# State tiles by twos and fours, attention heads by pairs, and the scaling of the weights on ScalarE, in a two-block model on one core

## The chip, the cores and the metric

The kernel runs on one core of a Trainium2 chip. A core has TensorE (PE in the profile, its weight loads PEld), VectorE (DVE), ScalarE (ACT), GpSimdE (POOL) and SyncE (SP), which here issues the transfers. The metric is the time of one execution on the device in microseconds (us); lower is better.

## The reference, cut to what matters

Two transformer blocks on 256 tokens of width 2048, one after the other. The change touches two parts of the second block's mixer, a diagonal state-space layer (64 groups of 16 channels, 64 complex states each) and an attention of 16 heads of 64 in four groups with three branches:

```python
def _s5(u, a_re, a_im, log_dt, b_re, b_im, c_re, c_im, d_skip):
    ...
    bu_re = jnp.einsum('btgc,gpc->tbgp', ug, bb_re)
    bu_im = jnp.einsum('btgc,gpc->tbgp', ug, bb_im)
    ...
    _, _, x_re, x_im = lax.associative_scan(_ssm_combine, (a_r, a_i, bu_re, bu_im), axis=0)
    y = (jnp.einsum('tbgp,gcp->btgc', x_re, c_re)
         - jnp.einsum('tbgp,gcp->btgc', x_im, c_im)
         + d_skip.reshape(SSM_GROUPS, SSM_GROUP) * ug)

def _nsa(q, kc_raw, vc_raw, ks_raw, vs_raw, kw_raw, vw_raw, g_logits, ...):
    k_cmp = _compress(kc_raw, cmp_pos, ck_w1, ck_w2)
    v_cmp = _compress(vc_raw, cmp_pos, cv_w1, cv_w2)
    ...
        o_c = jnp.einsum('bghqk,bkgd->bqghd', p_c.astype(v_cmp.dtype), v_cmp)
        ...
        p_s = _masked_softmax(s_s, (dist_s >= 0)[:, :, None])
        o_s = jnp.einsum('bghqk,bgqkd->bqghd', p_s.astype(vg.dtype), vg)
        ...
        p_w = _masked_softmax(s_w, valid_w)
        o_w = jnp.einsum('bghqk,bkgd->bqghd', p_w.astype(vwb.dtype), vwb)
        return gb[..., 0:1] * o_c + gb[..., 1:2] * o_s + gb[..., 2:3] * o_w
```

## The kernel before, in words

**The linears.** Every large product streams its weights in chunks of 512 KB (`chunk`, line 300): SP loads `wr` (4 buffers), ScalarE casts it to `wh` (3 buffers), VectorE subtracts and writes the residual `wl` (2 buffers). A chunk serves 24 matmuls of a full 128x128 array and 256 columns (high part by high part, residual by high, high by residual). After each chunk `linear` calls `background()`, which adds a share to every generator in the background and advances it a step when the sum reaches one. These matmuls read `wh` and `wl` with activations `r`, `m`, `hh` or `hl`; all matmuls go through `mm` and so have line 290 in before and 291 in the changed kernel.

**The state-space layer** (`s5`) runs in the background of the linears kv_in2, q_in2, gn_in2 and ga_in2 at 0.48 steps per chunk, 32 units j, one per step. A unit has two input matmuls with 32 rows of the array (`m,bt` in the profile, 256 columns, into a PSUM tile), six VectorE operations of 512 elements and two scans (`w<-ps,tab`, `w<-w,w`, `w<-mag,w`, `w<-w,tab`), and two steps later two output matmuls into 32 columns of the array (`w,cc`). Four units share the array's four row groups and column groups of 32, and one PSUM tile of outputs.

**The attention** (`nsa`) begins with the compressed branch: `compress` adds positions (`t<-m,params` and `t<-sw,params`, `sw` being a copy of the raw keys with the halves exchanged) and multiplies its own streamed weights. Then come 32 units, one head and branch each, at 0.75 steps per chunk behind the linears ga_in2, glu2 and gb_in2: `scores` (two matmuls on 64 rows, `m,m`; then VectorE's bias, maximum and sums, ScalarE's exponentials `w<-w,nm`, and VectorE's scaling `w<-w,sm` at line 282), two steps later `turn` (three transposes `eye,w` at line 1622 and a ScalarE copy to `pt`, which is `w<-ps 128x384`), and two steps after that `values` (two matmuls into 64 columns, `w,vt`; at a head's first branch also one on 15 rows, `pct,vcm`).

**What sets the order.** Each engine runs its instructions in one fixed order. The Tile scheduler decides that order from the program's order and its own model, so a step does not stand in one piece on an engine: instructions of a linear can stand between its matmuls. In the mixer, tiles `w` rotate in a ring of 11, `bt`, `cc`, `sw` and `tab` in rings of 2, PSUM tiles in 8 banks. A write into a ring's oldest buffer waits for its last reader.

Of the kernel before, what the change touches and what calls it, by code (L numbers as in the profile page):

```python
# [7 lines left out]
F32 = mybir.dt.float32  # L8
F32R = mybir.dt.float32r
ACT = mybir.ActivationFunctionType  # L10
ALU = mybir.AluOpType
# [3 lines left out]
P = 128  # L15
T = 256
# [4 lines left out]
EPS = 1e-6  # L21
NEG = -1e30
CH = 1024

# [202 lines left out]
class Builder:  # L227
# [1143 lines left out]
    def s5(self, pm, M, u):  # L1371
        nc = self.nc
        new = self.new
        sw = lambda a: a[:, ::-1]
        tiles = {}

        def load(c):
            bt = new(pm, "bt", [P, 2, P], F32, 2)
            nc.sync.dma_start(bt, self.d_bt[:, :, c * P:(c + 1) * P])
            cc = new(pm, "cc", [P, 2, P], F32, 2)  # L1380
            nc.sync.dma_start(cc[:, 0], self.ap["c_re"][:, c * P:(c + 1) * P])
            nc.sync.dma_start(cc[:, 1], self.ap["c_im"][:, c * P:(c + 1) * P])
            nc.gpsimd.tensor_scalar(out=cc[:, 1], in0=cc[:, 1], scalar1=-1.0, scalar2=None, op0=ALU.mult)
            tiles[c] = bt, cc

        def load_tab(j):

            tab = new(pm, "tab", [P, 3, T], F32, 2)
            nc.sync.dma_start(tab[:, 0:2], self.d_tab[j])
            self.act(tab[:, 2], tab[:, 1], ACT.Copy, scale=-1.0)  # L1390
            tiles["t", j] = tab

        def inputs(j):
            c, i = j // 4, j % 4
            sl = slice(32 * i, 32 * i + 32)
            bt = tiles[c][0]
            tab = tiles.pop(("t", j))
            cs = tab[:, 0:1].to_broadcast([P, 2, T])
            bu = self.ps()
            self.mm(bu[:, 0], bt[sl, 0], u[c][sl], True, True)  # L1400
            self.mm(bu[:, 1], bt[sl, 1], u[c][sl], True, True)
            p, r = new(pm, "w", [P, 2, T], F32, 11), new(pm, "w", [P, 2, T], F32, 11)
            self.tt(p, bu, cs, ALU.mult)
            self.tt(r, sw(bu), tab[:, 1:3], ALU.mult)
            self.tt(p, p, r, ALU.add)
            z = new(pm, "w", [P, 2, T], F32, 11)
            mg = self.mag[:, j:j + 1].to_broadcast([P, T])
            for k in range(2):
                nc.vector.tensor_tensor_scan(z[:, k], mg, p[:, k], 0.0, op0=ALU.mult, op1=ALU.add)
            x, r = new(pm, "w", [P, 2, T], F32, 11), new(pm, "w", [P, 2, T], F32, 11)  # L1410
            self.tt(x, z, cs, ALU.mult)
            self.tt(r, sw(z), tab[:, 2:0:-1], ALU.mult)
            self.tt(x, x, r, ALU.add)
            tiles["x", j] = x

        def outputs(j):
            c, i = j // 4, j % 4
            sl = slice(32 * i, 32 * i + 32)
            if i == 0:
                tiles["y"] = self.ps()[:, 0]  # L1420
            psy, cc, x = tiles["y"], tiles[c][1], tiles.pop(("x", j))
            self.mm(psy[sl], cc[:, 0, sl], x[:, 0], True, False, True)
            self.mm(psy[sl], cc[:, 1, sl], x[:, 1], False, True, True)
            if i < 3:
                return None
            y = self.t1()
            d = self.par("ssm_d_2")
            self.stt(y, u[c], d[:, c:c + 1], psy, ALU.mult, ALU.add)
            self.act(y, y, ACT.Gelu_apprx_tanh)
            hi, lo = M(F32R), M(F32R)  # L1430
            self.split(y, hi, lo)
            return hi, lo

        load(0)
        load_tab(0)
        for j in range(34):
            res = outputs(j - 2) if j >= 2 else None
            if j % 4 == 2 and j < 30:
                load(j // 4 + 1)
            if j < 31:  # L1440
                load_tab(j + 1)
            if j < 32:
                inputs(j)
            yield res

    def nsa(self, pm, M, q, kv, gates, onsa):
        nc, ap = self.nc, self.ap
        new = self.new
        kc, vc, ks, vs, kw, vw = (kv[2 * n:2 * n + 2] for n in range(6))
# [6 lines left out]
        ps = self.ps()  # L1456
# [35 lines left out]
        for which, raw in (("k", kc), ("v", vc)):  # L1492
# [1 line left out]
            hid = self.ps()[0:60, 0]  # L1494
            pos = self.par("cmp_pos_2")

            sw = new(pm, "sw", [P, 2, T], F32, 2)
            for t in range(2):
                nc.sync.dma_start(sw[64:128, t], raw[t][0:64])
                nc.sync.dma_start(sw[0:64, t], raw[t][64:128])  # L1500
# [77 lines left out]
                self.act(pct[j][:, sl], tp[:, j], ACT.Copy)  # L1578
        yield

        units = [(m, a, br) for m in range(8) for a in range(2) for br in range(2)]
        held = {}

        def scores(n):
            m, a, br = units[n]
            hi = (m % 4) * 4 + 2 * (m // 4) + a
            ds = slice(64 * a, 64 * a + 64)
            if br == 0:
                bias = new(pm, "w", [P, 3, P], F32, 11)

                nc.sync.dma_start(bias[:, 0], self.hankel(hi, P))
                nc.sync.dma_start(bias[:, 1:3].rearrange("p a b -> p (a b)"), self.hankel(hi, T))
                held["bias"] = bias
            bias = held["bias"]
            k = (ks, kw)[br][m // 4]
            ps = self.ps().rearrange("p a (b c) -> p (a b) c", c=P)
            self.mm(ps[:, 0:2].rearrange("p a b -> p (a b)"), q[m][ds, P:T], k[ds], True, True)
            self.mm(ps[:, 2], q[m][ds, 0:P], k[ds, 0:P], True, True, True)
            s = new(pm, "w", [P, 3, P], F32, 11)
# [12 lines left out]
            self.tt(sm, sm, gates[:, :, 16 * (br + 1) + hi], ALU.mult)  # L1612
            self.ts(s[:, 0:2], s[:, 0:2], sm[:, 1:2], None, ALU.mult)
            self.ts(s[:, 2], s[:, 2], sm[:, 0:1], None, ALU.mult)
            held["s", n] = s

        def turn(n):
            s = held.pop(("s", n))
            tp = self.ps().rearrange("p a (b c) -> p (a b) c", c=P)

            for b, src in enumerate((2, 0, 1)):
                nc.tensor.transpose(tp[:, b], s[:, src], self.eye)  # L1622
            pt = new(pm, "w", [P, 3, P], F32, 11)
            self.act(pt, tp[:, 0:3], ACT.Copy)
            held["p", n] = pt

        def values(n):
            m, a, br = units[n]
            g = 2 * (m // 4) + a
            ds = slice(64 * a, 64 * a + 64)  # L1630
            if a == 0 and br == 0:
                held["o"] = self.ps()[:, 0]
            o = held["o"]
            if br == 0:
                gs = slice(32 * g, 32 * g + 15)
                self.mm(o[ds], vcm[gs], pct[m % 4][gs], True, False, True)
            pt, vt = held.pop(("p", n)), vts[br]
            gc = slice(g * 64, g * 64 + 64)
            self.mm(o[ds], vt[:, 0, gc], pt[:, 0:2].rearrange("p a b -> p (a b)"), False, False, True)
            self.mm(o[ds, P:T], vt[:, 1, gc], pt[:, 2], False, br == 1, True)  # L1640
            if a == 1 and br == 1:
                hi, lo = M(F32R), M(F32R)
                self.split(o, hi, lo)
                onsa.append((hi, lo))

        for n in range(len(units) + 4):
            if n >= 4:
                values(n - 4)
            if 2 <= n < len(units) + 2:
                turn(n - 2)  # L1650
            if n < len(units):
                scores(n)
            yield

    def hankel(self, head, n):
# [46 lines left out]
```

## Time and profile before

| | |
|---|---|
| median of 3 runs | 3635.79 us (3632.27 to 3638.65) |
| the profiled execution | 3634.55 us |
| its span, first to last instruction | 3632.8 us |
| TensorE's granted clock, mean | 0.990 of full speed |
| TensorE busy | 3554.9 us |
| VectorE busy | 2220.6 us |
| ScalarE busy | 1580.4 us |

The span is what the profiler saw between the first and last instruction; 1.75 us lie around it. Busy times overlap between engines. The two parts that change lie between about 2116 and 2640 us of the span: the state-space layer up to some 2420 us, the attention's units behind it.

### The profile page before, as it was taken

The page shows a single profiled execution, that of the slowest core. Times are in us where ns is not written, and L with a number is a line of the kernel's source. Part 1 is how long each engine was busy: PE and PEld are TensorE (multiplying, and loading weights), DVE is VectorE, ACT ScalarE, POOL GpSimd, SP SyncE. Part 2 cuts the span into 40 slices and gives each one's busy share as a digit, 9 for nine tenths or more (in the row PEclk, how much of TensorE's full clock was granted, in tenths as well). Part 3 has the DMA queues.
Part 4 walks back from the last instruction along what each step waited for, and adds up shares of the span by engine and source line. Part 5 has one row for each costly group of instructions (what it writes and reads, how often), then busy time and mean ns, then how long its engine had stood idle before and what let it go on. Part 6 is the DMA issues. An engine that isn't in the chain of part 4 may idle for free.

```text
span 3632.8 us, 67934 instructions
## 1 busy us (share of the span) xinstructions
PE 3554.9 (98%) x28264; PEld 3372.4 (93%) x28264; DVE 2220.6 (61%) x3210; ACT 1580.4 (44%) x2033; POOL 20.0 (1%) x65
## 2 busy tenths in 40 slices
PE   8999999999999999999999899999999999999998
PEld 4788899999999999999999888888899899999997
DVE  2564367676655489865544689876656755555445
ACT  2433345454444444444434433455544544444333
POOL 0000000000000000000000000000000000000000
PEclk9999999999999999999999999999999999999999
DMA  9886857676555556765555555544455455555554
GB/s 340 312 287 215 289 187 231 220 229 214 184 182 185 182 188 221 225 197 185 182 185 181 165 167 176 163 150 126 122 177 185 151 186 181 185 182 184 182 184 140
DMA packets 213318, 710.83 MB, mean 196 GB/s; under 512 B 23904, under 2 KB 39296, under 8 KB 213008
## 3 DMA queue, kind: packets, MB, share of 16 engines
q1 hardware_dynamic: 213008, 706.48, 59.9%
q8 instruction: 221, 3.62, 0.4%
q14 instruction: 89, 0.73, 0.1%
HBM read 694.29 MB, written 11.57 MB: 194 GB/s over the span
## 4 chain that ended last, share of the span: by engine, by line
PE 94%; DVE 3%; DMA 1%; ACT 1%; issue 1%; SPq 0%; ACTq 0%; DVEq 0%
PE ps L290 93%; DVE wl L275 1%; DVE r L278 1%; DVE t L275 0%; PE ps L1622 0%; DMA wr<-in_w_qk_in 0%; DVE w L275 0%; DMA r<-in_xT 0%; DMA wr<-in_w_ada 0%; ACT wh L272 0%; DVE r L275 0%; DMA tab<-d_tab 0%; DVE t L278 0%; DMA wa<-in_w_qk_in 0%; DMA wa<-in_w_ada 0%
## 5 line engine op out<-in xcount | busy, mean ns | idle before, releaser
L275 DVE TENSOR_TENSOR wl<-wr,wh 128x1024 fp32r<-128x1024 f32 x1064 | 1300.6, 1223 | 1105.7 <-PE ps L290 869.4
L272 ACT ACTIVATE wh<-wr 128x1024 fp32r<-128x1024 f32 x1064 | 1127.0, 1059 | 1569.5 <-PE ps L290 1406.2
L290 PE MATMUL ps<-r,wh 128*128 128x256 f32 x12224 | 1759.9, 285 | 28.1 <-ACT r L272 22.0
L290 PEld LDWEIGHTS ps<-r,wh 128*128 128x128 f32 x12224 | 1592.7, 192 | 70.6 <-ACT r L272 28.4
L290 PE MATMUL ps<-r,wl 128*128 128x256 f32 x6112 | 998.4, 285 | 9.0 <-DVE wl L275 8.9
L290 PEld LDWEIGHTS ps<-r,wl 128*128 128x128 f32 x6112 | 847.8, 192 | 26.0 <-issue 12.3
L290 PE MATMUL ps<-hh,wl 128*128 128x256 f32 x2112 | 345.0, 283 | 0.0
L290 PE MATMUL ps<-hl,wh 128*128 128x256 f32 x2112 | 345.0, 283 | 0.0
L290 PE MATMUL ps<-hh,wh 128*128 128x256 f32 x2112 | 343.9, 283 | 0.0
L290 PEld LDWEIGHTS ps<-hh,wl 128*128 128x128 f32 x2112 | 294.0, 192 | 0.0
L290 PEld LDWEIGHTS ps<-hl,wh 128*128 128x128 f32 x2112 | 294.0, 192 | 0.0
L290 PEld LDWEIGHTS ps<-hh,wh 128*128 128x128 f32 x2112 | 293.4, 192 | 0.0
L290 PE MATMUL ps<-m,wh 128*128 128x256 f32 x1024 | 152.8, 286 | 0.0
L290 PEld LDWEIGHTS ps<-m,wh 128*128 128x128 f32 x1024 | 134.1, 191 | 7.0 <-issue 3.2
L290 PE MATMUL ps<-wr,silu_c 128*32 128x512 f32 x348 | 78.6, 618 | 9.2 <-DMA wr<-in_w_ada 9.2
L278 DVE SCALAR_TENSOR_TENSOR acc<-wr,silu_c,acc 128x1024 f32<-128x1024 f32 x50 | 64.1, 1283 | 36.3 <-DMA wr<-in_w_ada 36.1
L290 PE MATMUL ps<-m,wl 128*128 128x256 f32 x512 | 83.0, 284 | 0.0
L278 DVE SCALAR_TENSOR_TENSOR t<-ps,params,t 128x255 f32<-128x255 f32 x176 | 76.6, 475 | 0.6
L272 ACT ACTIVATE t<-ps 128x256 f32<-128x256 f32 (+2 forms) x87 | 39.4, 458 | 85.2 <-PE ps L290 65.3
L275 DVE TENSOR_TENSOR wl<-wa,wh 128x1024 fp32r<-128x1024 f32 (+1 forms) x34 | 40.8, 1199 | 58.0 <-ACT wh L272 30.0
L290 PEld LDWEIGHTS ps<-m,wl 128*128 128x128 f32 x512 | 70.4, 191 | 3.9 <-DVE wl L275 1.7
L272 ACT ACTIVATE t<-ps,params 128x256 f32<-128x256 f32 x88 | 46.6, 563 | 55.5 <-PE ps L290 34.7
(233 smaller groups left out, 1858.9 us busy)
## 6 DMA issues: line engine op xcount, KB each, us to landing
wr<-in_w_up SPq DMA_DIRECT2D x528, 512.0 KB, 3.6
wr<-in_w_down SPq DMA_DIRECT2D x264, 512.0 KB, 3.5
wr<-in_w_ada SPq DMA_DIRECT2D x141, 512.0 KB, 5.2
wr<-in_w_out SPq DMA_DIRECT2D x53, 512.0 KB, 3.8
wa<-in_w_ada SPq DMA_DIRECT2D x51, 512.0 KB, 5.2
wr<-in_w_ga_in SPq DMA_DIRECT2D x32, 512.0 KB, 3.7
wr<-in_w_glu SPq DMA_DIRECT2D x32, 512.0 KB, 3.5
wr<-in_w_gb_in SPq DMA_DIRECT2D x32, 512.0 KB, 3.5
```

The source lines that it names most:

```text
L272: return self.nc.scalar.activation(out=out, in_=in_, func=func, **kw)
L275: return self.nc.vector.tensor_tensor(out, a, b, op=op)
L278: return self.nc.vector.scalar_tensor_tensor(out=out, in0=a, scalar=s, in1=b, op0=op0, op1=op1)
L290: self.nc.tensor.matmul(out, lhsT, rhs, start=start, stop=stop, skip_group_check=skip)
```

## The change

`s5` now makes inputs for two units at once (k outside, the two units inside, a PSUM tile each) and outputs for four (k outside, the four column groups inside). Tables are loaded two units ahead. `nsa` takes the two heads of a tile m as one unit: 16 units of two heads, whose matmuls alternate between the halves of the array; a unit has two steps, the second with the turn; values come three units after scores rather than four. The two scalings of the weights become ScalarE copies with a scale. `bt` and `cc`, `sw` and all `w` share one ring of 15 buffers, where there were 11 and three rings of 2 (`bt` and `cc` of half the size).

```diff
+NW = 15
         def load(c):
-            bt = new(pm, "bt", [P, 2, P], F32, 2)
+            t = new(pm, "w", [P, 2, 2, P], F32, NW)
+            bt, cc = t[:, 0], t[:, 1]
...
+        def inputs(j0):
+
+            c = j0 // 4
             bt = tiles[c][0]
+            bus = [self.ps(), self.ps()]
+            for k in range(2):
+                for n in range(2):
+                    sl = slice(32 * (j0 % 4 + n), 32 * (j0 % 4 + n) + 32)
+                    self.mm(bus[n][:, k], bt[sl, k], u[c][sl], True, True)
+            tiles["bu"] = bus
...
+        def outputs(c):
+
+            psy, cc = self.ps()[:, 0], tiles[c][1]
+            xs = [tiles.pop(("x", 4 * c + i)) for i in range(4)]
+            for k in range(2):
+                for i in range(4):
+                    sl = slice(32 * i, 32 * i + 32)
+                    self.mm(psy[sl], cc[:, k, sl], xs[i][:, k], k == 0, k == 1, True)
...
         for j in range(34):
-            res = outputs(j - 2) if j >= 2 else None
             if j % 4 == 2 and j < 30:
                 load(j // 4 + 1)
-            if j < 31:
-                load_tab(j + 1)
             if j < 32:
-                inputs(j)
-            yield res
+                if j % 2 == 0:
+                    inputs(j)
+                states(j)
+                if j < 30:
+                    load_tab(j + 2)
+            yield outputs(j // 4 - 1) if j > 4 and j % 4 == 1 else None
...
-            sw = new(pm, "sw", [P, 2, T], F32, 2)
+            sw = new(pm, "w", [P, 2, T], F32, NW)
...
+            for ds, ps in zip(halves, pss):
+                self.mm(ps[:, 0:2].rearrange("p a b -> p (a b)"), q[m][ds, P:T], k[ds], True, True)
+            for ds, ps in zip(halves, pss):
+                self.mm(ps[:, 2], q[m][ds, 0:P], k[ds, 0:P], True, True, True)
+            held["s", n] = [weights(br, hi, ps, bias) for hi, ps, bias in zip(heads, pss, held["bias"])]
...
-            self.ts(s[:, 0:2], s[:, 0:2], sm[:, 1:2], None, ALU.mult)
-            self.ts(s[:, 2], s[:, 2], sm[:, 0:1], None, ALU.mult)
+            self.act(s[:, 0:2], s[:, 0:2], ACT.Copy, scale=sm[:, 1:2])
+            self.act(s[:, 2], s[:, 2], ACT.Copy, scale=sm[:, 0:1])
...
+            for ds, gc, pt in zip(halves, cols, pts):
+                self.mm(o[ds], vt[:, 0, gc], pt[:, 0:2].rearrange("p a b -> p (a b)"), False, False, True)
+            for ds, gc, pt in zip(halves, cols, pts):
+                self.mm(o[ds, P:T], vt[:, 1, gc], pt[:, 2], False, br == 1, True)
...
-        for n in range(len(units) + 4):
-            if n >= 4:
-                values(n - 4)
+        for n in range(len(units) + 3):
+            if n >= 3:
+                values(n - 3)
+            if n < len(units):
+                scores(n)
+            yield
             if 2 <= n < len(units) + 2:
                 turn(n - 2)
-            if n < len(units):
-                scores(n)
             yield
```

How this moves instructions is seen in the order on each engine. A row is an instruction with its place in the engine's order, line, output and inputs (name and number of the tile), and the output's partitions and elements; x2 stands for two alike in succession.

TensorE, early in the state-space layer, before: an output and an input of one unit each stand together, and further on inputs of two units.

```order
8935 L290 MATMUL ps_23617<-r_22633,wh_23620 128x256 x2
8936 L290 MATMUL ps_23550<-w_23485,cc_23385 32x256 x2
8937 L290 MATMUL ps_23653<-m_23033,bt_23383 128x256 x2
8938 L290 MATMUL ps_23616<-r_22640,wh_23671 128x256 x2
...
8951 L290 MATMUL ps_23617<-r_22654,wh_23701 128x256 x2
8952 L290 MATMUL ps_23734<-m_23035,bt_23553 128x256 x2
8953 L290 MATMUL ps_23822<-m_23035,bt_23553 128x256 x2
8954 L290 MATMUL ps_23616<-r_22654,wl_23702 128x256 x2
```

The same layer after: the shared tile of `bt` and `cc` is now a `w` (23552 and 23383). Inputs of two units alternate, but the first four units' eight output matmuls stand in three places.

```order
8930 L291 MATMUL ps_23725<-m_23035,w_23552 128x256
8931 L291 MATMUL ps_23726<-m_23035,w_23552 128x256
8932 L291 MATMUL ps_23725<-m_23035,w_23552 128x256
8933 L291 MATMUL ps_23726<-m_23035,w_23552 128x256
8934 L291 MATMUL ps_23823<-w_23408,w_23383 32x256
8935 L291 MATMUL ps_23823<-w_23484,w_23383 32x256
...
8988 L291 MATMUL ps_23823<-w_23571,w_23383 32x256
...
9000 L291 MATMUL ps_23823<-w_23657,w_23383 32x256
9001 L291 MATMUL ps_23823<-w_23408,w_23383 32x256
9002 L291 MATMUL ps_23823<-w_23484,w_23383 32x256
9003 L291 MATMUL ps_23823<-w_23571,w_23383 32x256
9004 L291 MATMUL ps_23823<-w_23657,w_23383 32x256
```

So the first k of the four units went to three places as their states became ready, and the second k of all four stands together.

VectorE, where `compress` adds positions. Before, these additions from `sw` stand early, with a residual `wl` between them:

```order
1770 L275 TENSOR_TENSOR wl_23702<-wr_23699,wh_23701 128x1024
...
1774 L275 TENSOR_TENSOR w_23657<-ps_23653,tab_23559 128x512
1775 L275 TENSOR_TENSOR t_3630_25374<-sw_25281,params_75 64x8x15 x4
1776 L275 TENSOR_TENSOR wl_23753<-wr_23750,wh_23752 128x1024
...
1782 L275 TENSOR_TENSOR t_3655_25511<-sw_25281,params_75 64x8x15 x4
...
1785 L275 TENSOR_TENSOR wl_23783<-wr_23780,wh_23782 128x1024
```

After, `sw` is a `w` of the ring (25274), and its additions stand some 200 instructions later, beside the states of two units:

```order
1971 L276 TENSOR_TENSOR wl_25462<-wr_25459,wh_25461 128x1024
...
1974 L276 TENSOR_TENSOR t_3625_25371<-w_25274,params_75 64x8x15 x2
...
1976 L276 TENSOR_TENSOR t_3625_25371<-w_25274,params_75 64x8x15 x2
1977 L1416 SCALAR_TENSOR_TENSOR w_25314<-mag_13783,w_25309 128x256 x2
...
1980 L276 TENSOR_TENSOR w_25318<-w_25314,tab_25113 128x512
...
1983 L276 TENSOR_TENSOR t_3649_25507<-w_25274,params_75 64x8x15 x4
...
1987 L276 TENSOR_TENSOR w_25443<-ps_25437,tab_25231 128x512
1991 L276 TENSOR_TENSOR wl_25480<-wr_25477,wh_25479 128x1024
```

Between these two residuals stand 19 rows with no other residual.

TensorE in the attention, before: a visit with values, transposes and scores of three single units.

```order
10001 L290 MATMUL ps_26964<-w_26813,vt_25188 64x256
10002 L290 MATMUL ps_26964<-w_26813,vt_25188 64x128
10003 L1622 MATMUL ps_26968<-eye_77,w_26821 128x128 x3
10004 L290 MATMUL ps_26977<-m_23956,m_24654 128x256
10005 L290 MATMUL ps_26977<-m_23956,m_24654 128x128
```

After, the matmuls of two heads alternate; in the second visit here a matmul of a linear stands between the two first halves of the values.

```order
10101 L291 MATMUL ps_27095<-w_27026,vt_25180 64x256
10102 L291 MATMUL ps_27095<-w_27020,vt_25180 64x128
10103 L291 MATMUL ps_27095<-w_27026,vt_25180 64x128
10104 L291 MATMUL ps_27102<-m_24303,m_24652 128x256
10105 L291 MATMUL ps_27103<-m_24303,m_24652 128x256
...
10142 L291 MATMUL ps_27095<-w_27172,vt_25239 64x256
10143 L291 MATMUL ps_27266<-m_23835,wh_27269 128x256
10144 L291 MATMUL ps_27095<-w_27178,vt_25239 64x256
10145 L291 MATMUL ps_27095<-w_27172,vt_25239 64x128
10146 L291 MATMUL ps_27095<-w_27178,vt_25239 64x128
```

Eight of the 16 pairs of values are parted in this way.

## Rows read from the trace of the kernel before

**Rows 1.** The page: busy time by engine, and the chain that ended last.
```profile
PE 3554.9 (98%) x28264; PEld 3372.4 (93%) x28264; DVE 2220.6 (61%) x3210; ACT 1580.4 (44%) x2033; POOL 20.0 (1%) x65
...
PE 94%; DVE 3%; DMA 1%; ACT 1%; issue 1%; SPq 0%; ACTq 0%; DVEq 0%
```

**Rows 2.** Windows: stretch, length, busy PE, PEld, DVE, ACT, POOL, clock, DMA, GB/s.
```profile
2116.00:2420.00 304.00, 292.18 (x2087) 253.19 (x2086) 277.77 (x429) 119.76 (x159) 4.82 (x10) 0.97 0.53 165
2420.00:2640.00 220.00, 220.00 (x1537) 189.44 (x1538) 140.74 (x377) 130.58 (x258) 0.00 (x0) 1.00 0.44 128
...
2161.40:2258.70 97.30, 93.50 (x645) 79.92 (x644) 90.83 (x137) 32.19 (x42) 2.03 (x3) 0.96 0.53 164
2258.70:2320.60 61.90, 55.67 (x390) 47.55 (x390) 52.39 (x81) 20.64 (x27) 1.06 (x2) 0.94 0.48 152
2320.60:2418.90 98.30, 96.51 (x718) 84.83 (x716) 89.91 (x145) 49.76 (x71) 1.73 (x5) 0.97 0.54 172
```

**Rows 3.** TensorE's timeline at one wait: start, us, instruction, count, idle time before.
```profile
2168.46 1.05 PE L290 MATMUL ps<-w,cc 128*32 128x256 f32 x4 [3.80 <-DVE w L275]
...
2171.10 1.22 PE L290 MATMUL ps<-r,wh 128*128 128x256 f32 x4
```

**Rows 4.** TensorE's timeline around inputs of one unit, then of two.
```profile
2116.02 0.64 PE L290 MATMUL ps<-r,wh 128*128 128x256 f32 x4
2116.59 1.12 PE L290 MATMUL ps<-m,bt 32*128 32x256 f32 x4
2117.65 0.74 PE L290 MATMUL ps<-r,wh 128*128 128x256 f32 x4
2118.23 0.64 PE L290 MATMUL ps<-r,wl 128*128 128x256 f32 x4
2118.70 0.52 PE L290 MATMUL ps<-r,wh 128*128 128x256 f32 x3
...
2144.14 1.14 PE L290 MATMUL ps<-m,bt 32*128 32x256 f32 x8
2145.21 0.74 PE L290 MATMUL ps<-r,wl 128*128 128x256 f32 x4
```

**Rows 5.** TensorE's timeline: outputs of one unit, and of two.
```profile
2149.71 1.05 PE L290 MATMUL ps<-w,cc 128*32 128x256 f32 x4
2150.69 0.74 PE L290 MATMUL ps<-r,wl 128*128 128x256 f32 x4
...
2279.77 1.06 PE L290 MATMUL ps<-w,cc 128*32 128x256 f32 x8
```

**Rows 6.** TensorE's timeline: scores of one unit, then values of two units of one head.
```profile
2431.12 0.92 PE L290 MATMUL ps<-m,m 64*128 64x256 f32 x4
2431.96 0.74 PE L290 MATMUL ps<-r,wh 128*128 128x256 f32 x4
...
2471.20 0.64 PE L290 MATMUL ps<-pct,vcm 15*64 15x256 f32 x2
2471.77 1.51 PE L290 MATMUL ps<-w,vt 128*64 128x256 f32 x8
```

**Rows 7.** VectorE's groups: the scalings (2420 to 2640 us), then, 2116 to 2420 us, residuals and additions.
```profile
L282 DVE TENSOR_SCALAR w<-w,sm 128x256 f32<-128x256 f32 x32 | 11.3, 352 | 0.9
L282 DVE TENSOR_SCALAR w<-w,sm 128x128 f32<-128x128 f32 x32 | 9.0, 281 | 0.0
...
L275 DVE TENSOR_TENSOR wl<-wr,wh 128x1024 fp32r<-128x1024 f32 x74 | 90.0, 1219 | 17.6 <-issue 10.5 <-PE ps L290 7.0
L275 DVE TENSOR_TENSOR w<-ps,tab 128x512 f32<-128x512 f32 x64 | 41.0, 683 | 1.1 <-PE ps L290 1.1
L275 DVE TENSOR_TENSOR t<-sw,params 64x120 f32<-64x120 f32 x16 | 5.2, 353 | 0.2
```

**Rows 8.** ScalarE's groups: a copy with a scale (2116 to 2420 us), the copies `pt` (2420 to 2640 us).
```profile
L272 ACT ACTIVATE tab<-tab 128x256 f32<-128x256 f32 x30 | 12.5, 417 | 54.2 <-DMA tab<-d_tab 46.0 <-DVE w L275 7.4 <-DVE m L275 0.8
...
L272 ACT ACTIVATE w<-ps 128x384 f32<-128x384 f32 x32 | 15.4, 481 | 14.1 <-PE ps L1622 14.1
```

More of the change, by code (lines that the diff above doesn't have):

```diff
@@ L1377, in load @@
         def load(c):
-            bt = new(pm, "bt", [P, 2, P], F32, 2)
+            t = new(pm, "w", [P, 2, 2, P], F32, NW)
+            bt, cc = t[:, 0], t[:, 1]
             nc.sync.dma_start(bt, self.d_bt[:, :, c * P:(c + 1) * P])
-            cc = new(pm, "cc", [P, 2, P], F32, 2)
             nc.sync.dma_start(cc[:, 0], self.ap["c_re"][:, c * P:(c + 1) * P])
@@ L1391, in load_tab, with states @@
             tiles["t", j] = tab
-        def inputs(j):
-            c, i = j // 4, j % 4
-            sl = slice(32 * i, 32 * i + 32)
+        def inputs(j0):
+            c = j0 // 4
             bt = tiles[c][0]
+            bus = [self.ps(), self.ps()]
[4 more added lines that the diff above has]
+            tiles["bu"] = bus
+        def states(j):
+            bu = tiles["bu"][j % 2]
             tab = tiles.pop(("t", j))
             cs = tab[:, 0:1].to_broadcast([P, 2, T])
[L1399 to L1402, printed above, removed]
+            p, r = new(pm, "w", [P, 2, T], F32, NW), new(pm, "w", [P, 2, T], F32, NW)
             self.tt(p, bu, cs, ALU.mult)
@@ L1405, in inputs @@
             self.tt(p, p, r, ALU.add)
-            z = new(pm, "w", [P, 2, T], F32, 11)
+            z = new(pm, "w", [P, 2, T], F32, NW)
             mg = self.mag[:, j:j + 1].to_broadcast([P, T])
@@ L1409, in inputs @@
                 nc.vector.tensor_tensor_scan(z[:, k], mg, p[:, k], 0.0, op0=ALU.mult, op1=ALU.add)
-            x, r = new(pm, "w", [P, 2, T], F32, 11), new(pm, "w", [P, 2, T], F32, 11)
+            x, r = new(pm, "w", [P, 2, T], F32, NW), new(pm, "w", [P, 2, T], F32, NW)
             self.tt(x, z, cs, ALU.mult)
@@ L1414, in inputs @@
             tiles["x", j] = x
[L1416 to L1425, printed above, removed]
+        def outputs(c):
[5 more added lines that the diff above has]
+                    self.mm(psy[sl], cc[:, k, sl], xs[i][:, k], k == 0, k == 1, True)
             y = self.t1()
@@ L1435, in s5 @@
         load_tab(0)
+        load_tab(1)
         for j in range(34):
-            res = outputs(j - 2) if j >= 2 else None
             if j % 4 == 2 and j < 30:
                 load(j // 4 + 1)
-            if j < 31:
-                load_tab(j + 1)
             if j < 32:
-                inputs(j)
-            yield res
+                if j % 2 == 0:
[4 more added lines that the diff above has]
+            yield outputs(j // 4 - 1) if j > 4 and j % 4 == 1 else None
     def nsa(self, pm, M, q, kv, gates, onsa):
@@ L1579, in nsa, with weights @@
         yield
-        units = [(m, a, br) for m in range(8) for a in range(2) for br in range(2)]
+        units = [(m, br) for m in range(8) for br in range(2)]
+        halves = slice(0, 64), slice(64, 128)
         held = {}
         def scores(n):
-            m, a, br = units[n]
-            hi = (m % 4) * 4 + 2 * (m // 4) + a
-            ds = slice(64 * a, 64 * a + 64)
+            m, br = units[n]
+            k = (ks, kw)[br][m // 4]
+            heads = [(m % 4) * 4 + 2 * (m // 4) + a for a in range(2)]
             if br == 0:
[L1589 to L1599, printed above, removed]
+                held["bias"] = []
+                for hi in heads:
+                    bias = new(pm, "w", [P, 3, P], F32, NW)
+                    nc.sync.dma_start(bias[:, 0], self.hankel(hi, P))
+                    nc.sync.dma_start(bias[:, 1:3].rearrange("p a b -> p (a b)"), self.hankel(hi, T))
+                    held["bias"].append(bias)
+            pss = [self.ps().rearrange("p a (b c) -> p (a b) c", c=P) for _ in range(2)]
+            for ds, ps in zip(halves, pss):
[3 more added lines that the diff above has]
+            held["s", n] = [weights(br, hi, ps, bias) for hi, ps, bias in zip(heads, pss, held["bias"])]
+        def weights(br, hi, ps, bias):
+            s = new(pm, "w", [P, 3, P], F32, NW)
             self.tt(s.rearrange("p a b -> p (a b)"), ps[:, 0:3].rearrange("p a b -> p (a b)"),
@@ L1612, in scores @@
             self.tt(sm, sm, gates[:, :, 16 * (br + 1) + hi], ALU.mult)
-            self.ts(s[:, 0:2], s[:, 0:2], sm[:, 1:2], None, ALU.mult)
-            self.ts(s[:, 2], s[:, 2], sm[:, 0:1], None, ALU.mult)
-            held["s", n] = s
+            self.act(s[:, 0:2], s[:, 0:2], ACT.Copy, scale=sm[:, 1:2])
+            self.act(s[:, 2], s[:, 2], ACT.Copy, scale=sm[:, 0:1])
+            return s
         def turn(n):
-            s = held.pop(("s", n))
-            tp = self.ps().rearrange("p a (b c) -> p (a b) c", c=P)
@@ L1621, in turn @@
[L1621 to L1625, printed above, removed]
+            pts = []
+            for s in held.pop(("s", n)):
+                tp = self.ps().rearrange("p a (b c) -> p (a b) c", c=P)
+                for b, src in enumerate((2, 0, 1)):
+                    nc.tensor.transpose(tp[:, b], s[:, src], self.eye)
+                pt = new(pm, "w", [P, 3, P], F32, NW)
+                self.act(pt, tp[:, 0:3], ACT.Copy)
+                pts.append(pt)
@@ L1627, in values @@
+            held["p", n] = pts
         def values(n):
[L1628 to L1631, printed above, removed]
+            m, br = units[n]
+            g0 = 2 * (m // 4)
+            if br == 0:
                 held["o"] = self.ps()[:, 0]
[L1633 to L1641, printed above, removed]
+                for a, ds in enumerate(halves):
+                    gs = slice(32 * (g0 + a), 32 * (g0 + a) + 15)
+                    self.mm(held["o"][ds], vcm[gs], pct[m % 4][gs], True, False, True)
@@ L1642, in values @@
+            o, pts, vt = held["o"], held.pop(("p", n)), vts[br]
+            cols = [slice((g0 + a) * 64, (g0 + a) * 64 + 64) for a in range(2)]
+            for ds, gc, pt in zip(halves, cols, pts):
+                self.mm(o[ds], vt[:, 0, gc], pt[:, 0:2].rearrange("p a b -> p (a b)"), False, False, True)
+            for ds, gc, pt in zip(halves, cols, pts):
+                self.mm(o[ds, P:T], vt[:, 1, gc], pt[:, 2], False, br == 1, True)
+            if br == 1:
                 hi, lo = M(F32R), M(F32R)
```

## The prediction

> **What bounds the kernel now.** I read the page first: TensorE is busy 98% of the span and the chain that ended last is TensorE for 94% of it [rows 1]. So what shortens TensorE's work shortens the kernel, unless another engine bounds the stretch. The windows say where one does [rows 2]. From 2420 to 2640 us, where the attention's units run, TensorE never stops (220.00 of 220.00 us, clock 1.00), with VectorE at 140.74 and ScalarE at 130.58: that stretch is TensorE's alone. From 2116 to 2420 us, beside the state-space layer, TensorE has 292.18 of 304.00 us at clock 0.97, and VectorE 277.77. TensorE still ends the stretch, but VectorE is 26 us behind, so TensorE's savings there soon meet VectorE, whose work this change hardly reduces. The reader should also see that TensorE stops in places and is slow afterwards: at 2168.46 us an output waits 3.80 us for a state from VectorE, and from 2171.10 four matmuls take 1.22 us rather than 0.64 [rows 3, 4], the lower clock level (1.2 GHz).
>
> **What a visit of small matmuls costs.** Matmuls of a linear start 0.12 us apart: four between 2118.23 and 2118.70 [rows 4]. Inputs of one unit stand between 2116.59 and 2117.65, so 1.06 us for two matmuls of two passes each; the whole visit costs 2118.23 - 2116.02 - 8 x 0.12 = 1.25 us. Inputs of two units, which the scheduler has put side by side at 2144.14, take 1.07 us, eight passes in the time of four. So the row groups do run together, at no price. Outputs of one unit take 0.98 us [rows 5], and eight passes of two units 1.06 us busy beside 1.05 for four: column groups run together as well, in one PSUM tile. Pairs on 64 rows or 64 columns are not in the trace; one unit's scores take 0.84 us and values of two units of one head, which share their columns, are not joined (eight passes 1.51 us) [rows 6]. Nearest are the groups of 32, so I take halves as joined; the other bound is that they save nothing.
>
> I write a matmul of 256 columns as 0.43 us (four passes take 0.86 of the 1.06), one of 128 as half, and each change of tile shape as 0.17 us, since a lone visit has (1.25 - 0.86)/2 = 0.19 and one with outputs less.
>
> **The change, part by part.** *TensorE, state-space layer.* Before there are 128 matmuls, of which four joined pairs of units save 8: 120 x 0.43 = 52 us. After, inputs take 34 turns of 0.43 us (16 visits, two of them split by the scheduler) and outputs 29 rather than the ideal 16, because in six of the eight sets the first k is issued as each state becomes ready, as the order shows. 63 turns are 27 us. Changes of shape fall from 99 to 72, 5 us. Saving: 25 + 5 = 30 us, spread over the stretch.
>
> *TensorE, attention.* Scores and values are 32 x 0.65 us each and `pct` 16 x 0.43: 48.5 us. After: scores 10.4, values 10.4 plus 8 x 0.43 for the eight parted pairs, `pct` 3.4: 27.7 us. Changes of shape fall from 133 to 85, 8 us. Saving 21 + 8 = 29 us; with halves not joined, 8 us.
>
> Trainium skill, "TensorE: Matmul & The Clock Gate", Part 3, says that matmuls stay in strict order. By it two units issued one after the other (x2, then x2) would overlap in one matmul only. The trace disagrees: at 2144.14 before's order has x2 and x2, and eight passes took the time of four. Only two of the 16 input visits after are in that order, so by the rule the saving would be 0.9 us less.
>
> *VectorE* loses the scalings in the attention, 11.3 + 9.0 = 20.3 us [rows 7], where it isn't the bound (140.74 of 220): worth nothing by itself. Its work in the state-space layer is the same in sum, but moves. I count its rows in both orders between the same residuals `wl`, since each chunk needs one. In 2161.4 to 2258.7 us, 18 fewer operations of 512 elements and four fewer scans; in 2258.7 to 2320.6 us as many more, and 12 of the additions of `compress` (0.353), which now wait for the shared ring. At 0.683 for operations and the same for scans (estimate) that is -15 and +15 + 4 + 1 = +20.
>
> *ScalarE* gains 64 copies. A copy with a scale of 256 elements takes 0.417 us [rows 8]; the shorter at most that: 32 x 2 x 0.417 = 27 us, at least half. It comes to about 155 of 200 us in that stretch and isn't the bound, but it is in order: `pt` copies, for which values wait, stand behind casts and exponentials. Between transposes and values there are now often 24 matmuls of a linear, 24 x 0.12 = 2.9 us, where before two steps lay. Two copies of 0.48 us [rows 8] must fit in, with a cast and sometimes exponentials ahead. Mostly they do; I give 6 us for those that don't (bounds 0 and 25). *Transfers*: the same number; some biases now wait for the ring, with weight loads behind them on SP, which run several chunks ahead. If that cover were gone, each wait would show as a stop on `wr`; I cost it at nothing.
>
> **The sum by stretch.** Each takes the larger of TensorE's and VectorE's work.
> - 2116 to 2161.4: VectorE has 44.7 of 46.5 us with the last microsecond of the stretch (304.00 less the three windows, 277.77 less their sum 233.13): -1.
> - 2161.4 to 2258.7: TensorE 93.50, less the slow time (0.04 x 97.3 = 3.9), less 9 of 32 units' saving (8.4) = 81.2. VectorE 90.8 - 15 = 76. So 81.5 instead of 97.3: -16.
> - 2258.7 to 2320.6: VectorE 52.4 + 20 = 72 against TensorE's 55.67 less 4. VectorE bounds; durations overlap a little at their ends, so 71.5 instead of 61.9: +10. TensorE will stop here, where 19 VectorE rows stand between two residuals.
> - 2320.6 to 2418.9: TensorE 96.51 - 8/32 x 30 = 89; VectorE 86 with its waits: 91 instead of 98.3: -7.
> - 2420 to 2640: -29 + 6 = -23.
>
> Together -37. The profiled execution's 3634.55 (span 3632.8, 1.75 around it) becomes 3597.5; it lay 1.24 under the median, so against the median 3635.79 it is about **3599 us**.
>
> **The rivals.**
> - *All of TensorE's saving shows* (chance 0.13). VectorE keeps up because it works ahead during linears and the additions of `compress` spread. Then -30 - 29 and the two stops and slow times, 0.03 x 304 = 9 us, less 6 for ScalarE: -62, 3574 us. For it: VectorE had idle time in 2258.7 to 2320.6. Against it: `wl` has two buffers, so VectorE can't be far ahead.
> - *The attention's gain is lost to ScalarE* (0.15). Values wait for `pt`: a wait of 1.3 us at each of 16 units takes 21 us, leaving -37 + 15 = -22 or, with one or two slow stretches after stops of 3 to 4 us, about -16: 3614 to 3620 us. For it: ScalarE already waited 14.1 us for transposes [rows 8], and now has 20 us more ahead of these copies. Against: TensorE never waited for it before.
> - *Halves of 64 aren't joined* (0.07). The attention saves 8 us rather than 29: -16, 3620 us. For it: no row shows such a pair. The Trainium skill, "TensorEngine Tiling (Array Packing)", Gotcha 1, says different row tiles cannot use one PSUM bank at once; only the `pct` pairs do that here, 8 x 0.43 = 3.4 us, and no run shows it.
> - *Slower* (0.06). The same 19 rows of VectorE, and waits for states by output sets of four, stop TensorE often, each stop followed by a slow stretch that loses 3 to 4 us (3.9 in the one window). Twelve such stops of 3 us and their slow time, 78 us, outweigh the 59 saved: 3655 us. It decides from some nine stops. For it: a state now has to wait until all four are there. Against it: sets have two or more steps of slack and their first k is issued early.
> - *Nothing changes* (0.04): VectorE bounds the whole layer and ScalarE the attention; -5, 3631 us.
>
> The forecast itself has 0.55, range 3588 to 3611. Together: 0.55 + 0.13 + 0.15 + 0.07 give faster 0.9; same (within 0.2%, some 7 us, what the three runs scatter by) 0.04; slower 0.06. The range that leaves two in ten out goes from 3576 to 3621 us: it holds the forecast, both losses in the attention and the upper part of the full saving.
>
> **What would show it.** Right: in the changed profile groups of `m,w` and `m,m` of the same count are shorter in time start to start (eight passes of scores in about 0.85 us, eight of outputs in about 1.0); the work of 2420 to 2640 us takes some 197 us, TensorE still at 1.00; VectorE near full in the layer, with a stop of several us on `wl` where the 19 rows stand, followed by the lower clock. Wrong: waits of TensorE on ScalarE's `w` longer than 6 us in the attention (ScalarE late), eight passes of scores in 1.5 us (not joined), many waits on `w` from VectorE (slower), or a layer with no stops at all (full saving).

## The result, and the profile after

The changed kernel takes 3592.36 us (median of 4 runs, 3591.34 to 3595.09) where the kernel before takes 3635.81: a ratio of 0.9879, 95% interval 0.9864 to 0.9894, or 38 to 49 us less. The profiled execution is the slowest of the four, 3595.09 us with a span of 3593.4; some 6 us of it were lost ahead of the stretches that change (they begin at 2122.5 us, before at 2116.3). I therefore compare stretches between the same residuals `wl` of the mixer.

The windows of the changed kernel, with the columns of [rows 2]. The second to the fourth are cut at the same residuals as its last three, the first and the fifth are the rest of the layer and the attention:

```profile
2122.50:2166.80 44.30, 44.03 (x348) 39.75 (x347) 43.49 (x65) 16.61 (x21) 0.62 (x1) 1.00 0.57 177
2166.80:2243.00 76.20, 76.20 (x613) 70.19 (x614) 75.45 (x112) 28.35 (x35) 2.27 (x3) 1.00 0.64 198
2243.00:2314.00 71.00, 59.65 (x428) 51.13 (x425) 68.70 (x116) 23.86 (x33) 4.49 (x3) 0.90 0.49 150
2314.00:2407.80 93.80, 87.83 (x690) 81.33 (x689) 87.76 (x144) 47.40 (x69) 1.69 (x5) 0.93 0.58 177
2407.80:2600.00 192.20, 192.20 (x1544) 172.48 (x1543) 121.12 (x309) 148.64 (x320) 0.00 (x0) 1.00 0.51 149
```

The kernel before, cut at the first and last of these residuals, has a layer of 302.6 us and an attention of 221.2:

```profile
2116.30:2418.90 302.60, 290.78 (x2081) 252.42 (x2079) 276.65 (x428) 118.80 (x157) 4.82 (x10) 0.97 0.53 166
2418.90:2640.10 221.20, 221.20 (x1543) 190.02 (x1543) 141.84 (x378) 131.54 (x259) 0.00 (x0) 1.00 0.43 128
```

So the layer takes 285.3 us after, 17.3 less, and the attention 192.2, 29.0 less. In the attention TensorE is busy all the time, before and after: what it lost of work, the kernel gained. In the layer VectorE's work is the same (275.4 us over the first four windows, 276.65 before), and it now fills 285.3 us to 97%. One of the four windows is longer than before, 71.00 against 61.90 us: there TensorE is busy 59.65 us at a clock of 0.90.

The waits of TensorE in the layer, longest first in total (us, count, longest), then ScalarE's timeline ahead of the longest and TensorE's at the two longest:

```profile
PE ps L291 <- DVE wl L276: 7.8, 8, 2.2
PE ps L1302 <- ACT t L273: 4.4, 1, 4.4
PE ps L291 <- ACT t L273: 4.0, 1, 4.0
...
2263.04 1.28 ACT L273 ACT_TABLE_LOAD   x1
2264.34 0.42 ACT L273 ACTIVATE t<-t 48x256 f32<-48x256 f32 x1
...
2264.80 0.32 PE L1302 MATMUL ps<-eye,t 48*128 48x48 f32 x2 [4.41 <-ACT t L273]
...
2265.84 1.05 PE L291 MATMUL ps<-r,wl 128*128 128x256 f32 x4
...
2299.27 0.47 PE L291 MATMUL ps<-wh,t 128*60 128x256 f32 x1 [4.00 <-ACT t L273]
```

No output waits for a state any more, as at 2168.46 us before [rows 3]. But the transposes of the gates and the first product of `compress` come late, because VectorE reaches what ScalarE's `t` needs late; at the gates VectorE's part ends at 2262.58 us, and ScalarE itself then needs 2.2 us more, 1.28 of them a table load. After that stop four matmuls take 1.05 us, not 0.64, the lower clock level (1.2 GHz).

Visits of joined matmuls (TensorE's timeline; a visit is a run of small matmuls between matmuls of a linear): outputs of four units and scores of two heads, then values of a pair that is parted by a matmul of a linear, `pct` of two heads, and values that are not parted:

```profile
2414.29 1.07 PE L291 MATMUL ps<-w,w 128*32 128x256 f32 x16
2415.29 0.92 PE L291 MATMUL ps<-m,m 64*128 64x256 f32 x8
2416.14 0.74 PE L291 MATMUL ps<-r,wh 128*128 128x256 f32 x4
...
2453.27 0.65 PE L291 MATMUL ps<-w,vt 128*64 128x256 f32 x2
2453.84 0.38 PE L291 MATMUL ps<-m,wh 128*128 128x256 f32 x1
2454.15 0.86 PE L291 MATMUL ps<-w,vt 128*64 128x256 f32 x6
2454.95 0.39 PE L291 MATMUL ps<-m,wh 128*128 128x256 f32 x1
...
2594.94 0.65 PE L291 MATMUL ps<-pct,vcm 15*64 15x256 f32 x4
2595.52 0.39 PE L291 MATMUL ps<-r,wh 128*128 128x256 f32 x1
...
2606.74 0.87 PE L291 MATMUL ps<-w,vt 128*64 128x256 f32 x8
2607.54 0.74 PE L291 MATMUL ps<-r,wh 128*128 128x256 f32 x4
```

Sixteen passes of outputs take 1.00 us from start to the next visit (four took 0.98 [rows 5]), eight of scores 0.85 (four took 0.84 [rows 6]), eight of values 0.80. Halves of 64 join as groups of 32 do. The parted pair needs 2454.95 - 2453.27 = 1.68 us, one matmul of a linear among it. Eight pairs are parted so, and two more by a matmul of scores.

Summed over the attention's stretch, each matmul from its start to the next start, scores fall from 27.1 to 14.7 us, values from 23.9 to 17.7, `pct` from 9.1 to 4.6 and transposes from 14.1 to 8.6; the matmuls of the linears stay at 145 (144.6 and 145.1). A few matmuls at the cuts aside, the 29 us are those of the joined matmuls and of the transposes, which now stand in sixes and not in threes.

ScalarE in the attention, with the new copies `w<-w,sm`:

```profile
L273 ACT ACTIVATE w<-w,sm 128x256 f32<-128x256 f32 x32 | 16.1, 502 | 0.0
L273 ACT ACTIVATE w<-ps 128x384 f32<-128x384 f32 x30 | 12.7, 475 | 0.0
L273 ACT ACTIVATE w<-w,sm 128x128 f32<-128x128 f32 x32 | 12.6, 394 | 0.0
```

The copies take 28.7 us, and `pt` has no idle time before it, where it had 14.1 [rows 8]. TensorE waits for neither.

### The profile page after: what moved, and what is told of

Its sections match the earlier page's. It is cut to its first block, busy times and chain, and to the rows that moved or that the text cites. A ratio compares the mean times of both kernels' runs of the same rounds, so it can differ in the third digit from the quotient of the medians.

```text
span 3593.4 us, 67935 instructions
## 1 busy us (share of the span) xinstructions
PE 3508.3 (98%) x28264; PEld 3349.0 (93%) x28264; DVE 2198.6 (61%) x3146; ACT 1594.4 (44%) x2096; POOL 23.8 (1%) x65
## 4 chain that ended last, share of the span: by engine, by line
PE 92%; DVE 4%; DMA 2%; issue 1%; ACT 1%; SPq 0%; DVEq 0%; ACTq 0%
PE ps L291 92%; DMA wr<-in_w_ada 1%; DVE wl L276 1%; DVE w L276 1%; DVE t L276 1%; DVE r L279 0%; DMA r<-in_xT 0%; PE ps L1637 0%; DVE r L276 0%; DVE w L1416 0%; DMA tab<-d_tab 0%; ACT wh L273 0%; DMA wr<-in_w_qk_in 0%; DMA wa<-in_w_out 0%; DVE rstd L417 0%
## 5 line engine op out<-in xcount | busy, mean ns | idle before, releaser
L291 PE MATMUL ps<-wr,silu_c 128*32 128x512 f32 x348 | 80.5, 630 | 11.8 <-DMA wr<-in_w_ada 11.7
```

The lines of the kernel that those rows point to most:

```text
L291: self.nc.tensor.matmul(out, lhsT, rhs, start=start, stop=stop, skip_group_check=skip)
```

## The experiments

My theory: the attention is bound by TensorE alone, so each matmul joined there counts in full and VectorE's relief counts nothing; the layer is bound by VectorE once TensorE's work falls, so only part of the saving shows. The rivals were that VectorE's relief makes the attention faster, that the late additions of `compress` cost the layer some 10 us, and that the alternating order is what joins the matmuls. Ratios are against the kernel before, run beside each; `...` marks what is left out of an edit.

**The scaling back on VectorE.**

```diff
-            self.act(s[:, 0:2], s[:, 0:2], ACT.Copy, scale=sm[:, 1:2])
-            self.act(s[:, 2], s[:, 2], ACT.Copy, scale=sm[:, 0:1])
+            self.ts(s[:, 0:2], s[:, 0:2], sm[:, 1:2], None, ALU.mult)
+            self.ts(s[:, 2], s[:, 2], sm[:, 0:1], None, ALU.mult)
```

Expected: 

> The changed kernel with the two scalings of the attention weights back on VectorE; all else is kept. Theory (TensorE alone bounds the attention stretch, and the joined pairs shorten it): VectorE gets 20 us of work back in a stretch of 192 us where it is busy 121, so the time stays at 3592 us, within 4, and the stretch stays at 192 us with TensorE at 100%. Rival (relief of VectorE made the attention faster): 10 to 20 us slower, 3602 to 3612.

Measured 3590.18 us, ratio 0.987 (0.9854 to 0.9885). The attention's window:

```profile
2401.80:2593.60 191.80, 191.61 (x1540) 171.73 (x1541) 136.18 (x375) 126.80 (x255) 0.00 (x0) 1.00 0.50 150
```

VectorE has 15 us more and ScalarE 22 less than with the change, and the stretch is 191.8 us instead of 192.2. So the rival fails: that part of the change moved work between two engines that both had time.

**`sw` in a ring of its own.**

```diff
-NW = 15
+NW = 13
-            sw = new(pm, "w", [P, 2, T], F32, NW)
+            sw = new(pm, "sw", [P, 2, T], F32, 2)
```

Expected: 

> The changed kernel with the compress copy sw back in a ring of its own (2 buffers) and 13 instead of 15 in the shared ring, the same memory. The order has its additions early again and VectorE's work between residuals 53 and 66 of the mixer falls from 68 to 55 us (row counts by durations). Theory (VectorE bounds this stretch because the additions came late): that stretch takes about 60 instead of 71 us, some of it comes back later, and the whole is 3583 us, 3578 to 3588. Rival (it is only the same work at another place, VectorE bounds the whole layer): 3592, within 3. Second rival (13 buffers are too few): slower than 3595.

Measured 3591.35 us, ratio 0.9872 (0.9858 to 0.9885): the first rival. The windows at the same residuals as above:

```profile
2114.10:2162.00 47.90, 45.70 (x347) 41.21 (x346) 46.39 (x76) 18.01 (x22) 0.85 (x1) 0.96 0.60 179
2162.00:2239.10 77.10, 77.10 (x614) 70.45 (x614) 76.12 (x114) 28.75 (x37) 4.91 (x3) 1.00 0.62 193
2239.10:2297.70 58.60, 54.02 (x413) 46.98 (x414) 54.78 (x86) 21.33 (x28) 0.53 (x1) 0.97 0.54 164
2297.70:2394.90 97.20, 91.03 (x677) 81.15 (x676) 91.30 (x146) 47.01 (x67) 8.44 (x6) 0.93 0.56 177
2394.90:2593.60 198.70, 197.46 (x1569) 177.09 (x1569) 127.97 (x325) 151.67 (x327) 0.00 (x0) 0.99 0.48 144
```

The third window falls from 71.0 to 58.6 us as forecast, 12.4 less. But the others give it back: 3.6, 0.9, 3.4 and 6.5 us. The late additions did lengthen that window, but moving them gains nothing: where they go early, other work goes late, some of it behind the last residual of the layer (VectorE has 127.97 us in the last window, not 121.12, with 396.6 over all five in both kernels). What the smaller ring, 13 for 15, adds to this was not run apart.

**Each part alone**, both with the shared ring and both edits against the changed kernel: the layer's steps as before and the attention as changed, then the reverse.

```diff
...
         for j in range(34):
+            res = outputs(j - 2) if j >= 2 else None
             if j % 4 == 2 and j < 30:
                 load(j // 4 + 1)
+            if j < 31:
+                load_tab(j + 1)
             if j < 32:
-                if j % 2 == 0:
-                    inputs(j)
-                states(j)
-                if j < 30:
-                    load_tab(j + 2)
-            yield outputs(j // 4 - 1) if j > 4 and j % 4 == 1 else None
+                inputs(j)
+            yield res
```

```diff
-        units = [(m, br) for m in range(8) for br in range(2)]
+        units = [(m, a, br) for m in range(8) for a in range(2) for br in range(2)]
...
-            self.act(s[:, 0:2], s[:, 0:2], ACT.Copy, scale=sm[:, 1:2])
+            self.ts(s[:, 0:2], s[:, 0:2], sm[:, 1:2], None, ALU.mult)
```

Expected of the first: 

> The changed kernel with the state-space layer's steps as before (inputs and outputs of one unit at a time), the attention by pairs, the scaling on ScalarE and the shared ring kept. Theory: the attention's 29 us stay, the layer takes what it took before or some us more since sw waits for the ring: 3607 us, 3602 to 3617. Rival (the gain hangs on both together, or on the layer): above 3620.

Expected of the second: 

> The changed kernel with the attention's units as before (one head, scaling on VectorE), the layer by twos and fours and the shared ring kept. Theory: the layer's 17 us stay, the attention's stretch is again 220 us with TensorE at 100%: 3619 us, 3613 to 3624. Rival (VectorE bounds the layer, so joined matmuls give nothing there): 3630 or more.

Measured 3616.08 us, ratio 0.994 (0.9927 to 0.9952), and 3616.82 us, ratio 0.9942 (0.993 to 0.9955). The attention's windows of the first and the second:

```profile
2422.90:2616.30 193.40, 193.40 (x1537) 172.88 (x1536) 121.19 (x310) 148.75 (x320) 0.00 (x0) 1.00 0.49 148
```

```profile
2402.50:2622.80 220.30, 220.11 (x1550) 189.62 (x1551) 140.29 (x375) 130.39 (x257) 0.00 (x0) 1.00 0.44 131
```

The parts add up: 22 and 21 us less, 43 with both. The attention changes from 221.2 to 193.4 us with the layer as it was, and the second's layer takes 284.5 us, as in the changed kernel (285.3). That the first is 22 and not 28 lies in the layer: with the shared ring its 2116 to 2422.9 us take 4 us longer than before.

**Partners one after the other.**

```diff
-            for k in range(2):
-                for n in range(2):
+            for n in range(2):
+                for k in range(2):
                     sl = slice(32 * (j0 % 4 + n), 32 * (j0 % 4 + n) + 32)
...
                 self.mm(ps[:, 0:2].rearrange("p a b -> p (a b)"), q[m][ds, P:T], k[ds], True, True)
-            for ds, ps in zip(halves, pss):
                 self.mm(ps[:, 2], q[m][ds, 0:P], k[ds, 0:P], True, True, True)
...
                 self.mm(o[ds], vt[:, 0, gc], pt[:, 0:2].rearrange("p a b -> p (a b)"), False, False, True)
-            for ds, gc, pt in zip(halves, cols, pts):
                 self.mm(o[ds, P:T], vt[:, 1, gc], pt[:, 2], False, br == 1, True)
```

Expected: 

> The changed kernel with the matmuls of inputs, scores and values written one partner after the other (both of the first, then both of the second) rather than in turns; outputs as in the change. In the order, the first and second partner then follow each other directly in values, and scores stand with one or no matmul between. Theory (partners join in whatever order they are issued, as 0.013 us between two units' first passes in the kernel before showed for x2, x2): 3592 us, within 5. Rival (matmuls start strictly in order, so only the second of one and the first of the other overlap): 0.43 us more for each of 16 scores and 16 values, 14 us and more, 3604 to 3612.

Measured 3583.52 us, ratio 0.985 (0.9835 to 0.9865), below the changed kernel, which neither side expected. A visit with values and the window of the attention:

```profile
2450.37 0.88 PE L291 MATMUL ps<-w,vt 128*64 128x256 f32 x8
2451.18 0.50 PE L291 MATMUL ps<-m,wh 128*128 128x256 f32 x2
...
2404.90:2590.50 185.60, 185.60 (x1543) 171.32 (x1542) 122.71 (x310) 148.63 (x320) 0.00 (x0) 1.00 0.51 155
```

TensorE's and PEld's busy time for the values alone (tile `vt`) in the attention's window, changed kernel first:

```profile
2407.80:2600.00 192.20, 19.45 (x120) 9.04 (x120) 0.00 (x0) 1.00 0.51 149
2404.90:2590.50 185.60, 13.16 (x120) 7.58 (x120) 0.00 (x0) 1.00 0.51 155
```

Eight passes, issued as 256 and 128 columns of one head and then of the other, take 0.81 us: they join. And in this order the scheduler puts nothing between them, so no values are parted. The attention loses another 6.6 us, and the values alone are busy 6.3 us less. That is what eight parted pairs cost at 1.68 - 0.80 = 0.88 us each, less the one matmul of 0.12 that has to run anyway (6.1).

**One VectorE addition less**, in the changed kernel and in the kernel before (`self.tt(x, x, r, ALU.add)` is removed; the outputs then lack a part of the state).

Expected of the changed kernel: 

> The changed kernel without the last VectorE addition of a unit's states (32 of 512 elements; the outputs read x without its second part, so this leaves out part of the computation). Theory (VectorE bounds the changed layer): 32 x 0.60 = 19 us less of its work; TensorE stopped 17.6 us in the layer and lost some 13 to the low clock, so most of the 19 shows: 3576 us, 3570 to 3582. Rival (TensorE bounds the layer): 3592, within 4.

Expected of the kernel before: 

> The kernel before without the same addition (again part of the computation is left out). Theory (TensorE bounds the layer before, with two stops on VectorE's states): at most the stops and their slow time go, 14 us, likely half: 3630 us, 3622 to 3636. Rival (VectorE bounds it in both): 19 us less, 3617 or lower.

Measured 3580.48 us, ratio 0.9841 (0.9828 to 0.9854), and 3627.55 us, ratio 0.9973 (0.9963 to 0.9982). The layer's windows:

```profile
2118.00:2387.60 269.60, 260.18 (x2076) 237.49 (x2075) 255.56 (x398) 117.36 (x158) 6.38 (x11) 0.98 0.59 186
```

```profile
2116.90:2409.40 292.50, 288.26 (x2079) 250.80 (x2078) 260.10 (x401) 117.00 (x157) 5.16 (x10) 0.98 0.54 171
```

With 19.9 us less for VectorE the changed layer is 15.7 us shorter (285.3 to 269.6). With 16.6 us less the layer before is 10.1 shorter: TensorE's idle time falls from 11.8 to 4.2 us (302.60 - 290.78, 292.50 - 288.26) and its clock rises from 0.97 to 0.98, some 3 us. So VectorE bounds the changed layer most of the time, and before it cost the stops and the slow time behind them.

**That addition on GpSimd.**

```diff
-            self.tt(x, x, r, ALU.add)
+            nc.gpsimd.tensor_tensor(x, x, r, op=ALU.add)
```

Expected: 

> The changed kernel with the last addition of a unit's states on GpSimd, which has next to nothing to do. Theory (VectorE bounds the layer): if GpSimd's additions slow nothing else, as in the run without them, 3578 us, 3572 to 3584. Rival (GpSimd's addition is much longer, so that states come late, or it slows VectorE beside it): 3592 or slower.

Measured 3579.76 us, ratio 0.985 (0.9837 to 0.9864). The addition and the residuals beside it (2110 to 2420 us):

```profile
L1420 POOL TENSOR_TENSOR w<-w,w 128x512 f32<-128x512 f32 x32 | 43.4, 1356 | 248.5 <-DVE w L276 221.6 <-PE ps L291 16.3 <-PE ps L1583 10.6
...
L276 DVE TENSOR_TENSOR wl<-wr,wh 128x1024 fp32r<-128x1024 f32 x83 | 106.0, 1279 | 15.7 <-PE ps L291 8.1 <-issue 3.8 <-ACT tab L273 2.4
```

In the changed kernel the residuals of these 310 us are:

```profile
L276 DVE TENSOR_TENSOR wl<-wr,wh 128x1024 fp32r<-128x1024 f32 x81 | 98.3, 1216 | 13.0 <-PE ps L291 11.3 <-issue 1.6
```

GpSimd needs 1.356 us for what VectorE does in 0.68, and VectorE's residuals go from 1.216 to 1.279 us, 5 us over 83. It is those beside an addition that are slowed: of the 74 that lie in the layer, 12 overlap one for a fifth of their time or more and take 1.54 us on average, the others 1.23. The layer is 279.3 us, 6 less than with the change, the attention 190.1. The addition itself now takes twice as long and the layer is still shorter, so it is VectorE's load that counts there and not the length of a unit's chain of operations.

**Both together, and with `sw` apart.**

```diff
-            for k in range(2):
-                for n in range(2):
+            for n in range(2):
+                for k in range(2):
...
-            self.tt(x, x, r, ALU.add)
+            nc.gpsimd.tensor_tensor(x, x, r, op=ALU.add)
```

The first has all edits of the run with partners one after the other and of the run with the addition on GpSimd, the second also this:

```diff
-NW = 15
+NW = 13
...
-            sw = new(pm, "w", [P, 2, T], F32, NW)
+            sw = new(pm, "sw", [P, 2, T], F32, 2)
```

Expected of the first: 

> The kernel of b1 (partners one after the other) with the last addition of the states on GpSimd as in b4. Theory (the one shortens the attention, which TensorE bounds, the other the layer, which VectorE bounds, so both add up): 3592 - 9 - 12.5 = 3571 us, 3565 to 3577. Rival (the gains are one and the same): 3580.

Expected of the second: 

> The kernel of c1 with the ring of its own for sw from a2. Theory (with less work on VectorE the early additions no longer cost elsewhere what they spare between residuals 53 and 66): 5 us under c1, 3566 us, 3560 to 3572. Rival (as in a2 the work is only moved): the same as c1 within 3.

Measured 3578.15 us, ratio 0.9837 (0.9824 to 0.9851), and 3580.78 us, ratio 0.9843 (0.983 to 0.9856). The first's windows of layer and attention:

```profile
2114.50:2394.80 280.30, 266.50 (x2080) 242.81 (x2078) 262.31 (x401) 117.28 (x160) 50.80 (x43) 0.96 0.58 179
2394.80:2579.70 184.90, 184.90 (x1535) 170.50 (x1534) 122.71 (x311) 147.31 (x319) 0.00 (x0) 1.00 0.52 155
```

The first lies outside my 3565 to 3577, and by the time alone the rival's 3580 isn't excluded. By the stretches of the profiled executions the gains do add up: the layer takes 280.3 us, as with the addition on GpSimd (279.3), the attention 184.9, as with partners one after the other (185.6), together 12.3 us less than the change (285.3 + 192.2). My 3571 had added two medians that were each some us lower than the windows bear out. A ring of its own for `sw` again gives nothing. The first has the lowest median here, though the intervals of it and of the two runs that it joins overlap.

## Why the prediction was right, and where it was off

The direction and size held: 3599 forecast, 3592.36 measured, within the range. By the windows the change saved 46.3 us (43.4 by the medians), where the sum had 37; two terms, of 6 and 5 us, were off in the same direction. The steps, against the windows:

- **Attention, -29 + 6 = -23.** The 29 us of TensorE's saving came to the microsecond (29.0). The 6 for a late ScalarE was the mis-sized term: it is 0. The copies cost slightly more than the bound (28.7 us against at most 27: a copy whose scale differs by partition takes 0.502 us, not the 0.417 of the copy of `tab` with a constant scale [rows 8]), but TensorE never waited for `pt`. The rival in which ScalarE takes the gain falls with it; so does that of halves that don't join (0.85 us for eight passes of scores).
- **2116 to 2161.4, -1.** It is -0.8 (44.30 against 45.1).
- **2161.4 to 2258.7, -16.** It is -21.1. VectorE's 76 us were right (75.45), TensorE's 81.2 was not: I took its joined matmuls off, but not those of the three units whose states I had counted out of this stretch for VectorE. Their matmuls, and nine of a linear, now stand elsewhere (613 matmuls here against 645). TensorE then had 76.20 us and ran beside VectorE to the end.
- **2258.7 to 2320.6, +10.** It is +9.1, with VectorE busy 68.70 of 71.00 us. The stops came, but not as I had them: the longest, 4.41 us, is at the gates. At the 19 rows (they lie between the residuals of 2294.32 and 2306.78 us) the stop of 4.00 is on ScalarE's `t`, which waits for additions among them, and the wait for `wl` behind them is only 1.16.
- **2320.6 to 2418.9, -7.** It is -4.5, with waits for `wl` and a clock of 0.93.
- **TensorE's saving in the layer, 30.** The sum counts four joined pairs before. The trace has four of inputs, one of outputs (2279.77 [rows 5]) and two half joined (2209.93 and 2216.93), so 116 turns of 0.43 us rather than 120, and 28 us. It changes nothing, since VectorE bounds most of this layer.
- **VectorE bounds the changed layer.** Shown by taking 19.9 us of its work away, which gave 15.7. The rival of the full saving (3574 us) fails here, and so do the slower one and that of no change: outputs by four never stopped TensorE for a state.
- **Strict order of matmuls.** The Trainium skill, "TensorE: Matmul & The Clock Gate", Part 3, says that matmuls start and end in strict order. By that rule, as I read it, the kernel with partners one after the other would be slower by 0.43 us a pair; it was faster, and its visits took 0.81 us, where alternating ones took 0.80. Nor did the `pct` pairs pay for sharing a PSUM tile: 0.58 us from 2594.94 to 2595.52 for two, where one before took 0.57 [rows 6]. The Trainium skill, "TensorEngine Tiling (Array Packing)", Gotcha 1, says that different row tiles cannot access the same PSUM bank at once; the trace doesn't bear that out for these pairs, whose outputs lie in different halves of the tile's partitions.

What stays open is which of the layer's remaining stops a better order would spare: moving the additions, with `sw` in its own ring, gained nothing in either kernel that had it.

## What to carry to other kernels

Count joined matmuls in full only where TensorE never stops; where a second engine is 10% behind, as VectorE was in the layer, look first at how much of its work goes away, and test it by taking some away. When a scheduler decides the order, look in the order itself whether partners still stand together: one foreign matmul between two halves cost 0.76 us, more than the pair had saved (busy 1.51 us before [rows 6], 0.87 joined). A long stop moved out of one place is no gain until the windows behind it are read too.

## What the hardware showed that I had not expected

In the traces, first passes on different halves or groups start 0.007 us apart when the matmuls alternate (2606.741 and 2606.748) and 0.013 to 0.014 when they are issued two and two (2450.374 and 2450.388 with partners one after the other), and either way the pair takes the time of one: 0.80 and 0.81 us for values of two heads, 0.85 for scores of two (0.84 for one). Four column groups with 16 passes take 1.00 us. That also holds into one PSUM tile, as with values, outputs and `pct`. GpSimd's addition of 512 elements takes 1.356 us, twice VectorE's 0.68, and VectorE's residuals that overlap one take 1.54 us rather than 1.23.
